# Two column blocks in turn and a bias by running sum: one change to a two-layer hybrid decoder kernel

## The chip, the cores and the metric

The kernel runs on one core of one Trainium2 chip. The time is the device time of one execution in microseconds; the figure to be predicted is the median over the runs of the changed kernel. Before the change three runs took 926.28, 926.46 and 927.83 us, so the median is 926.46.

The core has five engines that each work through a queue of their own in order: TensorE (PE) multiplies matrices into the accumulator memory PSUM, VectorE (DVE) and ScalarE (ACT) work element by element, GpSimd (POOL) here does a few small things and starts transfers, SyncE (SP) starts transfers. They wait for each other by semaphores.

## The reference

Two layers (DEPTH = 2) on x of 256 tokens by 2048 columns, all in float32. Each layer normalises x, multiplies it by one wide matrix w_in, and feeds the columns to four head groups of 512 columns with four heads each. The groups' outputs, each gated, are joined and multiplied by w_out (2048 x 2048), and the result is added to x.

```python
for l in range(DEPTH):
    h = rms_norm(x, norm_g[l]);  p = split_columns(h @ w_in[l])
    log_f = log_sigmoid(p["fox_f"] + fox_fb[l])          # (256, 4 heads)
    cum = cumsum(log_f, over tokens)
    # group 0, FoX: logit[t, s] = q_t.k_s / sqrt(128) + cum[t] - cum[s], causal, softmax, times v
    # group 1: difference of two softmax maps; group 2, MoBA: here plain causal attention
    # group 3, GLA: gated linear attention
    mixed = concat(group outputs, each times silu(gate))
    x = x + mixed @ w_out[l]
return rms_norm(x, final_norm_g)
```

With 256 tokens the MoBA group has a single block of keys, so it is plain causal attention with rotary positions. What matters for the change is the bias of FoX: the row t gets cum[t] added on all of its keys, and a softmax along a row doesn't feel what is the same on the whole row. So any form of the bias will do that has the right differences along s.

## The kernel before

**Steps.** All weights lie in DRAM in the order in which they are used. `_blocks` (L96) lists the column blocks: for each layer 17 blocks of w_in, then 4 blocks of w_out of 512 columns (the last one of the second layer is cut). `_steps` (L131) cuts every block into steps along the 2048 rows: a step of a 512-column block is two tiles of 128 rows, so a block has eight steps. In a w_out block the row tiles come in the order of the groups 3, 0, 1, 2 (GLA, FoX, difference, MoBA); the group that is finished last, MoBA, fills the last two steps. A block with a `turn` shares its time with others of the same turn: the first few blocks of each layer go quarter by quarter, since their input arrives by quarters. The blocks of w_out had no turn.

**One step.** SP loads 512 KB of weights into one of four buffers `raw`. ACT copies it, rounded to the format that PE multiplies fast, into `hi` (L401), DVE subtracts to get the rest `lo` (L404); four buffers of each. PE then makes twelve matmuls of 512 columns (`multiply`, L1192): for two row tiles and two halves of the tokens, hi weights by hi and lo input, lo weights by hi input. `prepare` runs three steps ahead of `multiply`. The sums of a block stay in one of two PSUM buffers `mm`; when the block is complete, its `done` function drains it. For w_out that is `residual` (L1015): in layer 0 the first two blocks are copied to xs by ACT and x is added later by a DMA, all others are added to xs by DVE. Then `make_hT` (L434) turns the new x for the next layer by way of DRAM, in passes that are counted.

**Tasks.** Everything else (rotary, softmax, GLA, splitting the results) is written as generators in the list `tasks`. After each step `tick` (L258) goes once over the list and lets each task run to its next `yield`; it breaks off when a rough account of DVE or ACT time says that these have more than their share, the account being filled by PE's work. So the order on every engine is settled when the program is written. If a step needs a group that no task has finished (`need`, L1288), passes are forced until it is there, without steps between them.

**Turns through DRAM.** `moved` (L297) writes a tile to DRAM from POOL's queue, yields, reads it back in four parts from the same queue, and then yields LAND = 5 times before anything uses it. `gate` of MoBA, q and k of all groups go this way.

**The tail of a group.** `attend_columns` (L791) waits for v and for the turned gate, yields, multiplies by v into a PSUM buffer `side` (two of these, shared by all tasks), yields, multiplies by the gate on DVE, yields, and `split_group` (L526) makes hi (ACT), yields, and lo (DVE): the tiles mTh and mTl.

**The bias before.** `fox_first` (L840) takes the four gate columns out of PSUM (`fx`, 128 tokens x 2 x 4 heads, bias fb added). `fox_forget` (L858) makes their log-sigmoid, times sqrt(128), splits it into hi and lo, and scales a constant 0/1 triangle by each of the columns (16 ACT copies); DVE spreads the second half's values over 128 columns. The class `Forget` (L819) then adds the bias by eight products with 0/1 matrices (`upto_r`, `ones_r`) into the same PSUM sums as q by k; `softmax` (L722) calls it ahead of each set of scores. After that DVE adds the causal mask `neg4` to the diagonal parts.

**GLA** (`gla`, L612) works in two pairs of heads; in each, DVE fills `ee` and `tq`, and 28 PE products (L685) take both `side` buffers.

Of the kernel before, what the change touches and what calls it, by code (L numbers as in the profile page):

```python
# [21 lines left out]
P = 128  # L22
# [4 lines left out]
H = 4  # L27
# [36 lines left out]
def _constants():  # L64

    i = np.arange(P)
    tables, at = {"f": [], "b": []}, {}

    def put(name, a, kind="f"):
        parts = tables[kind]  # L70
        at[name] = (sum(x.shape[1] for x in parts), a.shape[1])
        parts.append(np.ascontiguousarray(a, TYPES[kind]))

    put("ident", np.eye(P))
    put("after", (i[:, None] > i[None, :]))
    for name, half in (("rot_d", DIFF_HALF), ("rot_m", MOBA_HALF)):
        rot = 2 * half
        inv = np.float32(500000.0) ** (-np.arange(0, rot, 2, dtype=np.float32) / np.float32(rot))
        ang = np.arange(SEQ, dtype=np.float32)[:, None] * inv[None, :]
        cos, sin = np.cos(ang), np.sin(ang)  # L80
        both = np.concatenate([cos, cos, -sin, sin], 1).reshape(2, P, 4 * half)
        put(name, both.transpose(1, 0, 2).reshape(P, -1))
    put("upto", (i[:, None] <= i[None, :]), "b")
    put("neg", np.where(i[None, :] > i[:, None], NEG, 0.0), "b")
    masks = []
    for h in GLA_LEVELS:
        blk, second = i // (2 * h), (i // h) % 2 == 1
        masks.append(((blk[:, None] == blk[None, :]) & ~second[:, None])[:, second])
    put("masks", np.concatenate(masks, 1), "b")
    return {k: np.concatenate(v, 1) for k, v in tables.items()}, at  # L90
# [5 lines left out]
def _blocks():  # L96

    def block(w, l, c0, n, kind, groups=(0, 1, 2, 3), turn=None):
        kts = [g * 4 + i for g in groups for i in range(4)]
        return {"w": w, "l": l, "c0": c0, "n": n, "kind": kind, "kts": kts, "per": 4 if n * 4 <= STEP_W else 2, "turn": turn}  # L100

    out = []
    for l in range(DEPTH):
        for i, (c0, n) in enumerate((
            (COL["gla_a"], 264),
            (COL["gla_q"], 512),
            (COL["gla_g"] + 248, 264),
            (COL["gla_v"], 512),
            (COL["fox_v"] + 258, 258),
            (COL["fox_q"], 512),  # L110
            (COL["fox_k"], 512),
            (COL["diff_q"], 512),
            (COL["diff_k"], 512),
            (COL["fox_v"], 258),
            (COL["fox_g"], 512),
            (COL["diff_v"], 512),
            (COL["moba_q"], 512),
            (COL["moba_k"], 512),
            (COL["diff_g"], 512),
            (COL["moba_g"], 512),  # L120
            (COL["moba_v"], 512),
        )):
            out.append(block("w_in", l, c0, n, "rows", turn=l if i in ((0, 1, 2), (0, 2))[l] else None))
        for chunk in range(4):
            cut = l + 1 == DEPTH and chunk == 3
            out.append(block("w_out", l, chunk * 512, 256 if cut else 512, "rows", (3, 0, 1, 2)))
    out.append(block("w_out", DEPTH - 1, D - 256, 256, "apart", (3, 0, 1, 2)))
    return out


def _steps():  # L131

    steps, first = [], {}
    for i, b in enumerate(_blocks()):
        per, turn = b["per"], b["turn"]
        for j in range(0, KT, per):
            key = (i, 0, 0) if turn is None else (first.setdefault(turn, i), j // 4, i)
            steps.append((key, len(steps), {"block": i, "kts": b["kts"][j:j + per], "first": j == 0, "last": j + per == KT}))
    steps = [s for _, _, s in sorted(steps, key=lambda z: z[:2])]
    at = 0  # L140
    for s in steps:
        s["at"] = at
        at += P * len(s["kts"]) * _BLOCKS[s["block"]]["n"]
    return steps
# [61 lines left out]
def hybrid_trunk(  # L206
# [107 lines left out]
        return ct[:, o:o + n]  # L314

    ident = cst("ident")
    after = cst("after")
    turns = {k: cst(k).rearrange("p (m z w) -> p m z w", m=2, z=2) for k in ("rot_d", "rot_m")}
    masks = cp.tile([P, NL, 64], U8, name="masks")
    fb = cp.tile([P, DEPTH, H], F32, name="fb")  # L320
    gain = cp.tile([P, 2, DEPTH], F32, name="gain")
    wa = cp.tile([17, DEPTH, 256], F32, name="wa")
    upto_r = cp.tile([P, P], F32R, name="upto_r")
    ones_r = cp.tile([P, P], F32R, name="ones_r")
    neg_b = cp.tile([P, P], BF16, name="neg_b")
    neg4 = neg_b[:, None, :].to_broadcast([P, H, P])
    halfpow = cp.tile([P, 8], F32, name="halfpow")
# [21 lines left out]
    def constants():  # L349
# [3 lines left out]
        nc.scalar.dma_start(wa[16:17].rearrange("p l e -> p (l e)"), gla_ba.rearrange("(o l) e -> o (l e)", o=1))  # L353
        yield
        s = []
        for name in ("upto", "masks"):
            c, n = CAT[name]
            s.append(s4.get([P, n], BF16))
            nc.scalar.dma_start(s[-1], const_b[:, c:c + n])
        yield  # L360
        c, n = CAT["neg"]
        nc.scalar.dma_start(neg_b, const_b[:, c:c + n])
        nc.scalar.dma_start(fb.rearrange("p l h -> p (l h)"), bcast_rows(fox_fb, 0, DEPTH * H))
        yield
        lamt = s2.get([P, DEPTH, 4, 64])
        nc.scalar.dma_start(lamt.rearrange("p l a d -> p (l a d)"), bcast_rows(diff_lam, 0, DEPTH * 256))
        nc.scalar.dma_start(gain, norms_t)
        yield
        v_.tensor_copy(upto_r, s[0])
        v_.tensor_copy(masks.rearrange("p l t -> p (l t)"), s[1])  # L370
        v_.tensor_scalar(ones_r, ident, 0.0, 1.0, op0=OP.mult, op1=OP.add)
        s4.put(*s)
        ready.add("constants")
        yield
# [237 lines left out]
    def gla(l, an):  # L612
# [34 lines left out]
        for pair in range(2):  # L647
# [32 lines left out]
            v_.tensor_mul(ee[:, 0, NL], ee[:, 0, NL], kv[:, 0])  # L680
            v_.tensor_mul(ee[:, 1, NL], ee[:, 1, NL], qv[:, 1])
            yield
            both = yield from take_both()
            pcs = [z.rearrange("p (l x c) -> p l x c", l=NL + 1, x=2) for z in both]
            for m in range(2):  # L685
# [36 lines left out]
    def softmax(qT, kT, scale, su, forget):  # L722
# [3 lines left out]
        for m in range(2):  # L726
            for kt in range(m + 1):
                dst = S[m][:, kt]
                if forget is not None:
                    forget(dst, m, kt)  # L730
                for h in range(H):
                    matmul(dst[:, h], qT[:, m * H + h], kT[:, :, kt * H + h],
                           forget is None, forget is None or h == H - 1)
        s4.put(qT, kT)
        if forget is not None:
            forget.release()
        yield
        p = []
        for m in range(2):
            v_.tensor_add(S[m][:, m], S[m][:, m], neg4)  # L740
            mx = sm.tile([P, H], F32, name="mx")
            if m == 0:
                v_.tensor_reduce(mx, S[0][:, 0], axis=AX.X, op=OP.max)
# [72 lines left out]
        yield  # L816
        yield from split_group(l, gi, mixed, lambda: s4.put(mixed))

    class Forget:  # L819


        def __init__(self):
            self.fg, self.f1 = [], []

        def __call__(self, dst, m, kt):
            fg, f1 = self.fg, self.f1
            if m == kt:
                matmul(dst, upto_r, fg[0][:, m], True, False)
                matmul(dst, upto_r, fg[1][:, m], False, False)
            else:  # L830
                matmul(dst, ones_r, fg[0][:, 0], True, False)
                matmul(dst, ones_r, fg[1][:, 0], False, False)
                matmul(dst, upto_r, f1[0], False, False)
                matmul(dst, upto_r, f1[1], False, False)

        def release(self):
            s4.put(*self.fg)
            s2.put(*self.f1)

    def fox_first(l, ps):  # L840
        r = env["r", l]
        vn = s4.get([P, 2, GW])
        fx = sm.tile([P, 2, H], F32, name="fx", bufs=2)
        for m in range(2):
            v_.scalar_tensor_tensor(fx[:, m], ps[m][:, 254:258], r[:, m:m + 1], fb[:, l], op0=OP.mult, op1=OP.add)
            a_.activation(vn[:, m, 258:], ps[m][:, :254], AF.Copy, scale=r[:, m:m + 1])
        env["fox_v", l] = vn
        env["forget", l] = Forget()
        tasks.append(fox(l))
        tasks.append(fox_forget(l, fx, env["forget", l]))  # L850

    def fox_v(l, ps):
        r, vn = env["r", l], env["fox_v", l]
# [1 line left out]
            a_.activation(vn[:, m, :258], ps[m], AF.Copy, scale=r[:, m:m + 1])  # L855
        ready.add(("fox_v", l))

    def fox_forget(l, fx, forget):  # L858
        yield
        e = sm.tile([P, 2, H], F32, name="fe", bufs=2)  # L860
        f = sm.tile([P, 2, H], F32, name="f", bufs=2)
        yield from log_sigmoid(f, fx, e)
        v_.tensor_scalar(f, f, math.sqrt(HD), None, op0=OP.mult)
        yield
        fh = sm.tile([P, 2, H], F32R, name="fh", bufs=2)
        fl = sm.tile([P, 2, H], F32R, name="fl", bufs=2)
        hi_of(fh, f)
        lo_of(fl, f, fh)
        yield
        for part in (fh, fl):  # L870
            z = yield from s4.take([P, 2, H, P], F32R)
            pf = part.bitcast(F32)
            for m in range(2):
                for h in range(H):
                    a_.activation(z[:, m, h], after, AF.Copy, scale=pf[:, m, h:h + 1])
                yield
            forget.fg.append(z)
            y = yield from s2.take([P, H, P], F32R)
            v_.tensor_copy(y, pf[:, 1, :, None].to_broadcast([P, H, P]))
            forget.f1.append(y)  # L880
            yield
        ready.add(("forget", l))

    def fox(l):
# [443 lines left out]
```

## Time and profile before

| what | value |
| --- | --- |
| median of three runs | 926.46 us (926.28 to 927.83) |
| time of the profiled execution | 925.78 us |
| its span, first to last instruction | 924.0 us |
| granted TensorE clock, mean | 0.994 |
| matmuls | 4694 |
| HBM read, written | 178.79 MB, 15.20 MB |
| DMA mean over the span | 211 GB/s |

In the rows of a profile, L12 is line 12 of the kernel; nearly all ACT and DVE rows have L176 and nearly all matmuls L277, the lines of the helpers that record them, so they are told apart by their tiles ("out<-in"). "x24" is a count. A float32 matmul of 128 columns counts as two records. A bracket holds the idle time just before an instruction and who ended it. Matmuls overlap, so start times tell PE's pace better than durations do.

### The profile page before, as it was taken

The page shows a single profiled execution, that of the slowest core. Times are in us where ns is not written, and L with a number is a line of the kernel's source. Part 1 is how long each engine was busy: PE and PEld are TensorE (multiplying, and loading weights), DVE is VectorE, ACT ScalarE, POOL GpSimd, SP SyncE. Part 2 cuts the span into 40 slices and gives each one's busy share as a digit, 9 for nine tenths or more (in the row PEclk, how much of TensorE's full clock was granted, in tenths as well). Part 3 has the DMA queues.
Part 4 walks back from the last instruction along what each step waited for, and adds up shares of the span by engine and source line. Part 5 has one row for each costly group of instructions (what it writes and reads, how often), then busy time and mean ns, then how long its engine had stood idle before and what let it go on. Part 6 is the DMA issues. An engine that isn't in the chain of part 4 may idle for free.

```text
span 924.0 us, 12695 instructions
## 1 busy us (share of the span) xinstructions
PE 907.0 (98%) x4694; PEld 771.5 (83%) x4694; DVE 625.6 (68%) x967; ACT 506.4 (55%) x712; POOL 88.9 (10%) x145
## 2 busy tenths in 40 slices
PE   9999999999999999899999999999999999998996
PEld 7989888898888888788898887888888888887886
DVE  7656777787569578556755549867975885694562
ACT  6576773374554466346656575743645545743441
POOL 1010002220001121001200100012110012110000
PEclk9999999999999999999999999999999999999999
DMA  8776557767657768578855845867776576694652
GB/s 320 245 241 190 182 176 260 248 204 229 209 177 230 228 189 235 170 202 261 289 178 164 256 150 178 242 190 247 225 232 178 167 243 207 203 290 147 201 160 92
DMA packets 56865, 194.84 MB, mean 211 GB/s; under 512 B 8001, under 2 KB 8289, under 8 KB 56802
## 3 DMA queue, kind: packets, MB, share of 16 engines
q1 hardware_dynamic: 46048, 164.20, 55.6%
q0 software_dynamic: 9264, 28.32, 10.8%
q10 hardware_dynamic: 1490, 1.51, 0.6%
q8 instruction: 37, 0.61, 0.3%
q14 instruction: 26, 0.21, 0.1%
HBM read 178.79 MB, written 15.20 MB: 210 GB/s over the span
## 4 chain that ended last, share of the span: by engine, by line
PE 95%; DVE 2%; ACT 1%; issue 1%; DMA 0%; POOLq 0%; POOL 0%; DVEq 0%; SPq 0%; ACTq 0%
PE mm L277 86%; PE side L277 9%; ACT eight L176 0%; DMA four<-in_xt 0%; DVE tq L176 0%; DVE lo L176 0%; ACT hi L176 0%; DVE mTl L176 0%; DVE four L176 0%; ACT mTh L176 0%; DVE xs L176 0%; ACT L176 0%; PE side L281 0%; DVE hTp L176 0%; POOLq L1324 0%
## 5 line engine op out<-in xcount | busy, mean ns | idle before, releaser
L176 DVE TENSOR_TENSOR lo<-raw,hi 128x1024 fp32r<-128x1024 f32 (+3 forms) x301 | 364.6, 1220 | 251.8 <-ACT hi L176 250.3
L176 ACT ACTIVATE hi<-raw 128x1024 fp32r<-128x1024 f32 (+3 forms) x301 | 317.1, 1059 | 362.3 <-PE mm L277 310.0
L277 PE MATMUL mm<-hi,hTp 128*128 128x512 f32 (+2 forms) x2048 | 465.1, 371 | 0.0
L277 PEld LDWEIGHTS mm<-hi,hTp 128*128 128x128 f32 x2048 | 358.3, 188 | 66.0 <-ACT hi L176 1.0
L277 PE MATMUL mm<-lo,hTp 128*128 128x512 f32 (+2 forms) x1024 | 249.8, 369 | 0.1
L277 PEld LDWEIGHTS mm<-lo,hTp 128*128 128x128 f32 x1024 | 181.1, 188 | 32.8 <-DVE lo L176 0.3
L277 PE MATMUL mm<-hi,mTh 128*128 128x512 f32 (+1 forms) x256 | 96.7, 382 | 4.8 <-ACT mTh L176 4.8
L277 PE MATMUL mm<-hi,mTl 128*128 128x512 f32 (+1 forms) x256 | 97.0, 383 | 1.5 <-DVE mTl L176 1.5
L277 PE MATMUL mm<-lo,mTh 128*128 128x512 f32 (+1 forms) x256 | 64.4, 376 | 0.0
L277 PEld LDWEIGHTS mm<-hi,mTh 128*128 128x128 f32 x256 | 49.0, 192 | 14.0 <-ACT mTh L176 5.2
L277 PEld LDWEIGHTS mm<-hi,mTl 128*128 128x128 f32 x256 | 49.2, 192 | 11.2 <-DVE mTl L176 2.1
L304 POOL DMA_DIRECT2D four<-turn x84 | 46.0, 553 | 102.2 <-DMA turn<-four 43.5
L277 PEld LDWEIGHTS mm<-lo,mTh 128*128 128x128 f32 x256 | 46.4, 189 | 8.9
L301 POOL DMA_DIRECT2D turn<-four x21 | 12.2, 582 | 407.9 <-DVE four L176 407.9
L176 DVE STREAM_TRANSPOSE pT<-four 32x128 f32<-32x128 f32 (+1 forms) x116 | 39.3, 350 | 1.0
L176 ACT ACTIVATE four<-mm,rstd 128x512 f32<-128x512 f32 (+2 forms) x56 | 33.6, 648 | 3.6 <-DVE fx L176 3.6
L176 ACT ACT_TABLE_LOAD x24 | 30.8, 1283 | 3.3 <-DVE an L176 3.0
L277 PEld LDWEIGHTS side<-four,four 128*128 128x128 f32 (+1 forms) x224 | 22.0, 190 | 2.3 <-issue 1.4
L277 PE MATMUL side<-four,four 128*128 128x128 f32 (+1 forms) x224 | 23.3, 277 | 0.0
L176 DVE STREAM_TRANSPOSE four<-four 128x1024 f32<-128x1024 f32 x18 | 22.4, 1245 | 0.3
L176 ACT ACTIVATE four<-side,nb 128x256 f32<-128x256 f32 (+1 forms) x48 | 20.5, 444 | 0.6 <-DVE nb L176 0.6
L176 DVE COPY_PREDICATED four<-masks,side 128x128 f32<-128x128 uint8 x56 | 19.0, 340 | 1.8
(145 smaller groups left out, 545.1 us busy)
## 6 DMA issues: line engine op xcount, KB each, us to landing
raw<-in_weights SPq DMA_DIRECT2D x272, 512.0 KB, 4.1
turn<-four POOLq DMA_DIRECT2D x21, 512.0 KB, 5.0
four<-turn POOLq DMA_DIRECT2D x84, 128.0 KB, 4.4
raw<-in_weights SPq DMA_DIRECT2D x16, 516.0 KB, 4.9
raw<-in_weights SPq DMA_DIRECT2D x15, 528.0 KB, 4.9
turn<-gate POOLq DMA_DIRECT2D x4, 512.0 KB, 4.8
gate<-turn POOLq DMA_DIRECT2D x16, 128.0 KB, 5.3
four<-in_xt SPq DMA_DIRECT2D x3, 512.0 KB, 7.1
```

The lines of the kernel that those rows point to most:

```text
L176: return f(*args, **kw)
L277: t_.matmul(out, lhsT, rhs, start=start, stop=stop)
L301: g_.dma_start(via, t.rearrange("p c a b -> p c (a b)"))
L304: g_.dma_start(t[c * 32:(c + 1) * 32].rearrange("p q a b -> p q (a b)"), via[:, c].rearrange("(q i) e -> i q e", q=4))
```

## The change

Three things are changed.

The first two blocks of w_out of each layer get a turn of their own with one cut, at row tile 12 of 16: first twelve row tiles (six steps) of block 0, then six steps of block 1, then the last two steps of block 0 and the last two of block 1. Blocks 2 and 3 follow as before.

FoX's bias is made in another way. PE transposes fx to four rows of 256 tokens, DVE adds fb (now one value per row), the log-sigmoid follows, DVE makes a running sum along the 256 keys and scales it by -sqrt(128). POOL's queue writes these 4 KB to DRAM and reads them back spread over 128 partitions (512 KB). DVE adds the causal mask to both diagonal parts in SBUF. In the softmax DVE adds the three resulting tiles to the scores, where it used to add the mask to two parts; the eight 0/1 products, the class Forget and the constants `after`, `upto` and `ones_r` are gone.

gla() gets one more yield in each pair, between its last multiplications on DVE and its taking both side buffers.

```diff
-            out.append(block("w_in", l, c0, n, "rows", turn=l if i in ((0, 1, 2), (0, 2))[l] else None))
+            out.append(block("w_in", l, c0, n, "rows", turn=(l, (4, 8, 12)) if i in ((0, 1, 2), (0, 2))[l] else None))
         for chunk in range(4):
             cut = l + 1 == DEPTH and chunk == 3
-            out.append(block("w_out", l, chunk * 512, 256 if cut else 512, "rows", (3, 0, 1, 2)))
+            out.append(block("w_out", l, chunk * 512, 256 if cut else 512, "rows", (3, 0, 1, 2),
+                             turn=(DEPTH + l, (12,)) if chunk < 2 else None))
...
-            key = (i, 0, 0) if turn is None else (first.setdefault(turn, i), j // 4, i)
+            key = (i, 0, 0) if turn is None else (first.setdefault(turn[0], i), sum(j >= c for c in turn[1]), i)
...
-    fb = cp.tile([P, DEPTH, H], F32, name="fb")
+    fb = cp.tile([H, DEPTH], F32, name="fb")
...
             v_.tensor_mul(ee[:, 1, NL], ee[:, 1, NL], qv[:, 1])
             yield
+            yield
             both = yield from take_both()
...
                 dst = S[m][:, kt]
-                if forget is not None:
-                    forget(dst, m, kt)
                 for h in range(H):
-                    matmul(dst[:, h], qT[:, m * H + h], kT[:, :, kt * H + h],
-                           forget is None, forget is None or h == H - 1)
+                    matmul(dst[:, h], qT[:, m * H + h], kT[:, :, kt * H + h], True, True)
...
-            v_.tensor_add(S[m][:, m], S[m][:, m], neg4)
+            if forget is None:
+                v_.tensor_add(S[m][:, m], S[m][:, m], neg4)
+            elif m == 0:
+                v_.tensor_add(S[0][:, 0], S[0][:, 0], forget[0])
+            else:
+                for j, z in enumerate(forget[1:]):
+                    v_.tensor_add(S[1][:, j], S[1][:, j], z)
+                s4.put(env["forget tile"])
+                s2.put(forget[0])
...
-            v_.scalar_tensor_tensor(fx[:, m], ps[m][:, 254:258], r[:, m:m + 1], fb[:, l], op0=OP.mult, op1=OP.add)
+            v_.tensor_scalar(fx[:, m], ps[m][:, 254:258], r[:, m:m + 1], None, op0=OP.mult)
...
+    def fox_forget(l, fx):
+        yield
+        ps = yield from take_side()
+        for m in range(2):
+            transpose(ps[0:H, m * P:(m + 1) * P], fx[:, m])
+        yield
+        z = yield from s2.take([P, SEQ])
+        e = yield from s2.take([P, SEQ])
+        v_.tensor_scalar(z[:H], ps[:H, :SEQ], fb[:, l:l + 1], None, op0=OP.add)
+        side.put(ps)
+        yield
+        yield from log_sigmoid(z[:H], z[:H], e[:H])
+        v_.tensor_tensor_scan(e[:H], z[:H], z[:H], 0.0, op0=OP.add, op1=OP.bypass)
+        v_.tensor_scalar(z[:H], e[:H], -math.sqrt(HD), None, op0=OP.mult)
+        s2.put(e)
+        yield
+        via = dram.tile([H, SEQ], F32, name="sums", tag="sums", bufs=2)
+        g_.dma_start(via, z[:H])
+        s2.put(z)
+        yield
+        t = yield from s4.take([P, H, SEQ])
+        g_.dma_start(t, via[None, :, :].to_broadcast([P, H, SEQ]))
+        for _ in range(LAND):
+            yield
+        first = yield from s2.take([P, H, P])
+        v_.tensor_add(first, t[:, :, :P], neg4)
+        v_.tensor_add(t[:, :, P:], t[:, :, P:], neg4)
+        env["forget tile"] = t
+        env["forget", l] = first, t[:, :, :P], t[:, :, P:]
         ready.add(("forget", l))
```

More of the change, by code (lines that the diff above doesn't have):

```diff
@@ L74, in _constants @@
     put("ident", np.eye(P))
-    put("after", (i[:, None] > i[None, :]))
     for name, half in (("rot_d", DIFF_HALF), ("rot_m", MOBA_HALF)):
@@ L82, in _constants @@
         put(name, both.transpose(1, 0, 2).reshape(P, -1))
-    put("upto", (i[:, None] <= i[None, :]), "b")
     put("neg", np.where(i[None, :] > i[:, None], NEG, 0.0), "b")
@@ L316, in hybrid_trunk @@
     ident = cst("ident")
-    after = cst("after")
     turns = {k: cst(k).rearrange("p (m z w) -> p m z w", m=2, z=2) for k in ("rot_d", "rot_m")}
     masks = cp.tile([P, NL, 64], U8, name="masks")
-    fb = cp.tile([P, DEPTH, H], F32, name="fb")
+    fb = cp.tile([H, DEPTH], F32, name="fb")
     gain = cp.tile([P, 2, DEPTH], F32, name="gain")
     wa = cp.tile([17, DEPTH, 256], F32, name="wa")
-    upto_r = cp.tile([P, P], F32R, name="upto_r")
-    ones_r = cp.tile([P, P], F32R, name="ones_r")
     neg_b = cp.tile([P, P], BF16, name="neg_b")
@@ L355, in constants @@
         s = []
-        for name in ("upto", "masks"):
+        for name in ("masks",):
             c, n = CAT[name]
@@ L362, in constants @@
         nc.scalar.dma_start(neg_b, const_b[:, c:c + n])
-        nc.scalar.dma_start(fb.rearrange("p l h -> p (l h)"), bcast_rows(fox_fb, 0, DEPTH * H))
+        nc.scalar.dma_start(fb, bass.AP(tensor=fox_fb.tensor, offset=fox_fb.offset, ap=[[1, H], [H, DEPTH]]))
         yield
@@ L368, in constants @@
         yield
-        v_.tensor_copy(upto_r, s[0])
-        v_.tensor_copy(masks.rearrange("p l t -> p (l t)"), s[1])
-        v_.tensor_scalar(ones_r, ident, 0.0, 1.0, op0=OP.mult, op1=OP.add)
+        v_.tensor_copy(masks.rearrange("p l t -> p (l t)"), s[0])
         s4.put(*s)
@@ L728, in softmax @@
                 dst = S[m][:, kt]
-                if forget is not None:
-                    forget(dst, m, kt)
                 for h in range(H):
-                    matmul(dst[:, h], qT[:, m * H + h], kT[:, :, kt * H + h],
-                           forget is None, forget is None or h == H - 1)
+                    matmul(dst[:, h], qT[:, m * H + h], kT[:, :, kt * H + h], True, True)
         s4.put(qT, kT)
-        if forget is not None:
-            forget.release()
         yield
@@ L817, in attend_columns @@
         yield from split_group(l, gi, mixed, lambda: s4.put(mixed))
[L819 to L838, printed above, removed]
     def fox_first(l, ps):
@@ L844, in fox_first @@
         for m in range(2):
-            v_.scalar_tensor_tensor(fx[:, m], ps[m][:, 254:258], r[:, m:m + 1], fb[:, l], op0=OP.mult, op1=OP.add)
+            v_.tensor_scalar(fx[:, m], ps[m][:, 254:258], r[:, m:m + 1], None, op0=OP.mult)
             a_.activation(vn[:, m, 258:], ps[m][:, :254], AF.Copy, scale=r[:, m:m + 1])
         env["fox_v", l] = vn
-        env["forget", l] = Forget()
         tasks.append(fox(l))
-        tasks.append(fox_forget(l, fx, env["forget", l]))
+        tasks.append(fox_forget(l, fx))
     def fox_v(l, ps):
@@ L856, in fox_v @@
         ready.add(("fox_v", l))
-    def fox_forget(l, fx, forget):
+    def fox_forget(l, fx):
         yield
[L860 to L863, printed above, removed]
+        ps = yield from take_side()
+        for m in range(2):
+            transpose(ps[0:H, m * P:(m + 1) * P], fx[:, m])
         yield
[L865 to L868, printed above, removed]
+        z = yield from s2.take([P, SEQ])
+        e = yield from s2.take([P, SEQ])
+        v_.tensor_scalar(z[:H], ps[:H, :SEQ], fb[:, l:l + 1], None, op0=OP.add)
+        side.put(ps)
         yield
[L870 to L880, printed above, removed]
-            yield
+        yield from log_sigmoid(z[:H], z[:H], e[:H])
[10 more added lines that the diff above has]
+        for _ in range(LAND):
+            yield
+        first = yield from s2.take([P, H, P])
[3 more added lines that the diff above has]
+        env["forget", l] = first, t[:, :, :P], t[:, :, P:]
         ready.add(("forget", l))
```

## The prediction

> **What bounds the kernel now.** I read the page first (busy times and the chain of waits), then the waits of PE, then the PE timeline around each wait.
>
> ```profile
> span 924.0 us, 12695 instructions
> PE 907.0 (98%) x4694; PEld 771.5 (83%) x4694; DVE 625.6 (68%) x967; ACT 506.4 (55%) x712; POOL 88.9 (10%) x145
> ...
> PE 95%; DVE 2%; ACT 1%; issue 1%; DMA 0%; POOLq 0%; POOL 0%; DVEq 0%; SPq 0%; ACTq 0%
> ```
>
> PE sets the time nearly everywhere. Only two things can move it: fewer matmuls, or fewer moments in which PE stands still. The waits of PE name the second:
>
> ```profile
> PE mm L277 <- ACT mTh L176: 4.8, 2, 2.4
> PE mm L277 <- DVE mTl L176: 1.5, 2, 0.8
> PE side L342 <- DVE four L337: 1.3, 1, 1.3
> PE side L277 <- DVE eight L176: 0.8, 1, 0.8
> ```
>
> The first two rows are one event in each layer, the third is the start of the program, the fourth a place in layer 1. The PE timeline shows what each costs (start, us, what; the bracket is the idle time before):
>
> ```profile
> 332.50 2.84 PE L277 MATMUL side<-four,four 128*128 128x128 f32 x24
> ...
> 337.03 1.08 PE L277 MATMUL mm<-lo,hTp 128*128 128x512 f32 x4
> 337.95 1.98 PE L277 MATMUL mm<-hi,hTp 128*128 128x512 f32 x8
> 339.76 1.07 PE L277 MATMUL mm<-lo,hTp 128*128 128x512 f32 x4
> 340.67 1.98 PE L277 MATMUL mm<-hi,hTp 128*128 128x512 f32 x8
> ...
> 381.47 2.84 PE L277 MATMUL side<-pT,four 128*128 128x128 f32 x24
> 386.71 0.51 PE L277 MATMUL mm<-hi,mTh 128*128 128x512 f32 x1 [2.40 <-ACT mTh L176]
> 387.97 0.80 PE L277 MATMUL mm<-hi,mTl 128*128 128x512 f32 x1 [0.76 <-DVE mTl L176]
> ...
> 391.06 1.07 PE L277 MATMUL mm<-lo,mTh 128*128 128x512 f32 x4
> ...
> 835.61 2.84 PE L277 MATMUL side<-pT,four 128*128 128x128 f32 x24
> ...
> 845.12 1.09 PE L277 MATMUL mm<-lo,mTh 128*128 128x512 f32 x4
> ```
>
> An undisturbed step is 2.72 us (337.95 to 340.67): 1.81 of "hi" matmuls, 0.91 of "lo". From the start of 24 side matmuls to the next "lo" it is 337.03 - 332.50 = 4.53. Around the wait in layer 0 the same work takes 391.06 - 381.47 = 9.59, in layer 1 845.12 - 835.61 = 9.51. So **each stall costs 5.06 and 4.98 us, together 10.04**, although PE is idle for only 2.40 + 0.76 = 3.16. The rest is a slow clock behind it: from 387.97 the last seven of the eight hi matmuls take 3.09 us to the next lo, 0.44 each, where eight in 1.81 are 0.23 each, and the window view (columns: span, busy time of PE, PEld, DVE, ACT, POOL, granted clock, DMA share, GB/s) has a clock of 0.76:
>
> ```profile
> 384.00:391.10 7.10, 3.94 (x12) 2.82 (x12) 2.45 (x2) 1.06 (x1) 0.00 (x0) 0.76 0.25 76
> ```
>
> **Part 1, two column blocks in turn.** The stall is the tail of the MoBA group. Its product with v (24 side matmuls), the gating, the split into hi and lo follow each other with nothing between, just ahead of the seventh step of the first w_out block, which needs them:
>
> ```profile
> 384.35 1.22 DVE L176 TENSOR_TENSOR four<-side,gate 128x1024 f32<-128x1024 f32 x1 [1.27 <-PE side L277]
> 386.69 1.23 DVE L176 TENSOR_TENSOR mTl<-four,mTh 128x1024 fp32r<-128x1024 f32 x1 [1.12 <-ACT mTh L176]
> ...
> 385.60 1.06 ACT L176 ACTIVATE mTh<-four 128x1024 fp32r<-128x1024 f32 x1 [3.78 <-DVE four L176]
> ...
> 356.79 2.18 POOL L304 DMA_DIRECT2D gate<-turn  x4 [2.92 <-DMA turn<-gate]
> ```
>
> The new order puts six steps of the second block ahead of that seventh step: 6 x 2.72 = 16.3 us and six passes of tick(). The tail needs five passes once the gate's turned tile counts as ready (attend_columns: one yield, product, gating, hi, lo). The gate's reads were issued at 356.79, nine steps before 381.47, and need five passes; passes that break off on the DVE budget can eat four of the nine. If none is owed, the tail ends one pass before it is needed, two steps ahead of PE; with one owed, in time still, because DVE runs ahead of PE. I cost the stall at nothing from here: gain 10.04. The other end is that all passes are still forced: gain 0.
>
> What is late next: the first block ends after 14 of the pair's 16 steps, 6 steps later than now (the last quarters of both stand at the end), so both PSUM buffers of "mm" are open at once, and the third block needs the first one's buffer two steps (5.44 us) after its last matmul. Draining it takes two instructions, behind one hi or one lo:
>
> ```profile
> L176 ACT ACTIVATE hi<-raw 128x1024 fp32r<-128x1024 f32 x268 | 282.7, 1061 | 324.4 <-PE mm L277 281.9 <-DMA raw<-in_weights 13.8 <-DVE four L176 6.4
> ...
> L176 DVE TENSOR_TENSOR lo<-raw,hi 128x1024 fp32r<-128x1024 f32 x268 | 325.0, 1221 | 221.4 <-ACT hi L176 220.2
> ...
> L176 DVE TENSOR_TENSOR xs<-mm,xs 128x512 f32<-128x512 f32 x10 | 6.4, 682 | 0.0
> ```
>
> Layer 1 (DVE): 1.22 + 2 x 0.68 = 2.6 us; layer 0 does it on ACT, whose copy of that size I take as no longer than DVE's: 1.06 + 1.36 = 2.4. Spare 2.8 us. I take 0; if it is missed by another 5 us of work ahead on that engine, PE idles 2.2 and loses about 3.6 by the ratio above (5.02 for 3.16). Then make_hT(0) of layer 0, with its x accumulation and turn on POOL's queue, starts 6 steps later than now, one block less ahead of make_hT(1), which keeps its place; layer 1's first steps come 18 steps (49 us) after the first block's end, and 13 passes are needed. Cost 0. Bytes of weights are the same, only their order differs.
>
> **Part 2, the bias.** Eight matmuls of 512 columns per layer go:
>
> ```profile
> 176.84 0.64 PE L277 MATMUL side<-four,upto_r 128*128 128x512 f32 x2
> ...
> 183.24 1.08 PE L277 MATMUL mm<-lo,hTp 128*128 128x512 f32 x4
> ...
> 636.42 0.64 PE L277 MATMUL side<-four,upto_r 128*128 128x512 f32 x2
> ...
> 642.82 1.08 PE L277 MATMUL mm<-lo,hTp 128*128 128x512 f32 x4
> ...
> 58.42 0.22 PE side L281 x2
> ```
>
> From the first forget matmul to the next "lo" is 6.40 us in both layers; MoBA's scores, the same without bias, take 4.53. Gain 2 x 1.87 = 3.74. Added are two transposes per layer, like the pair of GLA's in the last row: 2 x 0.22 = 0.44 of PE. Net gain 3.30, all of it on PE's path.
>
> The other engines:
>
> ```profile
> L176 ACT ACTIVATE four<-ct,fh 128x128 fp32r<-128x128 f32 x16 | 5.1, 389 | 0.0
> ...
> L176 DVE TENSOR_TENSOR side<-side,neg_b 128x512 f32<-128x512 f32 x12 | 8.3, 690 | 0.6 <-PE side L277 0.6
> ...
> L176 DVE TENSOR_TENSOR_SCAN two<-two 128x128 f32<-128x128 f32 x8 | 2.7, 404 | 0.0
> L176 DVE COPY at<-side 16x256 f32<-16x256 f32 x2 | 0.8, 405 | 0.0
> ...
> L176 DVE CAST two<-fh 128x512 fp32r<-128x512 f32 x2 | 0.8, 419 | 0.0
> ```
>
> ACT loses 16 scaled copies per layer (some 5 us). DVE loses two casts (0.84) and a few tiny instructions (about 0.5); it gains two mask additions in SBUF and one more on the scores (3 x 0.69), three passes over 4x256 (about 0.41 each, estimated from the 16x256 copy) and a scan of 256 (at most 2 x 0.404): 4.1. Net about +2.8 us of DVE per layer. It hides under PE, since DVE is 68% busy; uncovered it would cost 2 x 2.8 = 5.6.
>
> The way through DRAM is new on POOL's queue: a 4 KB write, then a broadcast read of 512 KB that waits for it. Behind them on that queue stand the turns of fox_q and fox_k, for which the projections' tasks count six passes (16.3 us). No row has this broadcast; the nearest are a 512 KB write and the broadcast of final_norm_g:
>
> ```profile
> turn<-four POOLq DMA_DIRECT2D x21, 512.0 KB, 5.0
> two<-in_final_norm_g POOLq DMA_DIRECT2D x4, 256.0 KB, 7.3
> ```
>
> The read is issued one pass (2.72 us) after the write, so it leaves at most 2.3 us late and lands 9.6 us after its pass; DVE's additions come five passes (13.6 us) after it. Spare 4.0 us. Twice 7.3 for twice the bytes would be 3.3 us late; the usual lead of DVE over PE (three steps, 8.2 us, less 2.3 for hi and lo) covers that. A turn held up behind them for the 5.0 us of the write still has room: two transfers of 5.0 in 16.3. I take 0 for all of it. The constants that go (a table of 64 KB, two small DVE instructions, half of a load on ACT's queue) stood beside the first blocks; 0.
>
> **Part 3, one more yield in gla().** The fourth wait:
>
> ```profile
> 561.64 1.07 PE L277 MATMUL mm<-lo,hTp 128*128 128x512 f32 x4
> 563.47 3.39 PE L277 MATMUL side<-tq,eight 128*128 128x128 f32 x28 [0.76 <-DVE eight L176]
> ```
>
> The side matmuls could have begun at 561.64 + 0.91 = 562.55; 0.92 us are lost because DVE is less than one step behind. A pass more is 2.72 us: gain 0.92, between 0 and 0.92. GLA's later end (two passes per layer) is far ahead of w_out.
>
> **Sum.** 10.04 + 3.30 + 0.92 = 14.26. The profiled execution took 925.78 us (span 924.0 and 1.78 around it): 911.52. The median of the runs is 0.68 above it, so 912.2.
>
> **A rule weighed.** The row first: PE idled 3.16 us in two pieces and the clock fell to 0.76 over the next microseconds. The Trainium skill, page "TensorE: Matmul & The Clock Gate" (What's actually happening; HAM oscillation), says the clock halves after an idle window of about 3.4 us and that gaps need only be kept below that. By that rule a wait this short would not by itself slow the clock, the slow stretch could have another cause and stay, and the sum would keep only the idle time. The trace disagrees as far as it goes: both stalls show the slow stretch, and it begins right behind them.
>
> **Rivals.** *The stall stays or moves (13%).* The tail is forced all the same, or the third block waits for its buffer. For: passes can break off on the budget, and both buffers are open. Against: 16.3 us of cover, 2.8 spare. One layer kept: 917.2; both: 922.2; buffers late in both layers by 3.6: 919.4.
> *The slow clock stays (4%).* Only the idle 2 x 3.16 = 6.32 of the 10.04 is won: 912.2 + 3.7 = 915.9. Against: the 0.76 us wait at 563.47 had no slow matmuls behind it, the longer ones had.
> *DVE work comes uncovered (3%).* 912.2 + 5.6 = 917.8.
> *Slower: the broadcast lands late (4%).* DVE works in order; waiting for the bias it holds back every "lo" behind it, and PE stops in fox's stage of each layer. It begins to cost when the read takes over 13.6 - 2.3 + 5.9 = 17.2 us, and eats the whole gain at about 5.3 us of idle (7.1 lost with the slow clock) per layer, so from 22.5 us on. At 25 us: 7.8 idle and 1.9 of slow clock, 9.7 per layer: 912.2 + 19.4 = 931.6. For: 128 partitions read the same 4 KB. Against: final_norm_g's broadcast does that too, at 7.3.
>
> **Chances.** The forecast holds at 76%. Below it little can lie: the remaining PE waits are the program's start, so 910.0 allows 2 us for what I rounded and for the runs' own spread. Above, 917.5 takes in one stall kept, the clock and the DVE case; it leaves out the two stalls kept, the late buffers and the slower case, some 12%, and what I haven't seen. About 0.2% (1.9 us) is what can be told from no change; faster: 95%, within: 1%, slower: 4%.
>
> **What would show it.** Right: no PE wait on mTh or mTl in the waits, the 24 matmuls of side<-pT between two steps of block 1 of w_out, granted clock 1.00 there; no groups with upto_r and ones_r, two transposes out of fx per layer; no wait of PE on "eight"; the first lo after fox's scores 4.5 us after their start. Wrong: PE waiting on the draining of mm (ACT or DVE xs) at the third block, a DVE wait on the broadcast's DMA with PE idle behind it, or new waits of PE on "lo" in the stages of GLA and FoX.

## The result and the profile after

Four executions of the changed kernel took 911.41, 912.68, 917.53 and 917.98 us, median 915.11; before, four took 926.00 to 927.83, median 926.37. The ratio is 0.987, 95% interval 0.984 to 0.990: faster by 1.3%. The forecast was 912.2 with a range of 910.0 to 917.5. The four times are two pairs some 5 us apart, and the forecast met the lower one. The median 915.11 is the mean of 912.68 and 917.53, a time that no execution took; with three long ones of four it would have left the range, so that it lies inside is partly luck. Most of what follows is about the gap.

The profiled execution took 912.68 us, 13.10 less than that of before. Busy times from its page:

```profile
PE 899.6 (99%) x4682; PEld 766.5 (84%) x4682; DVE 630.8 (69%) x969; ACT 498.0 (55%) x678; POOL 91.4 (10%) x149
```

The waits of PE, all of them:

```profile
PE side L338 <- DVE four L333: 1.3, 1, 1.3
PE side L280 <- issue: 1.0, 1, 1.0
PE side L280 <- DVE xs L175: 0.2, 1, 0.2
```

The rows on mTh, mTl and "eight" are gone; the program's start is left, and a new place has come: the eight transposes (L280) of the last quarter of x between the layers, which wait 1.02 and 0.25 us. The PE timeline of the same profile shows the places that the sum was made of:

```profile
179.36 2.84 PE L276 MATMUL side<-four,four 128*128 128x128 f32 x24
...
183.89 1.08 PE L276 MATMUL mm<-lo,hTp 128*128 128x512 f32 x4
...
384.84 2.84 PE L276 MATMUL side<-pT,four 128*128 128x128 f32 x24
...
389.34 1.07 PE L276 MATMUL mm<-lo,mTh 128*128 128x512 f32 x4
...
561.88 1.07 PE L276 MATMUL mm<-lo,hTp 128*128 128x512 f32 x4
562.79 3.29 PE L276 MATMUL side<-tq,eight 128*128 128x128 f32 x28
...
830.22 2.84 PE L276 MATMUL side<-pT,four 128*128 128x128 f32 x24
...
834.72 1.07 PE L276 MATMUL mm<-lo,mTh 128*128 128x512 f32 x4
```

From MoBA's product with v to the next lo it is 4.50 us in both layers (9.59 and 9.51 before), FoX's scores take 4.53 (6.40), and GLA's products follow their step after exactly the 0.91 us of its lo. So the gains stand: 10.10, 3.74 less the new transposes, 0.92. The new place takes some of it back. The PE timeline at the change of layers, after and then before:

```profile
457.66 1.14 PE L276 MATMUL side<-lo,hTp 128*128 128x264 f32 x8
459.82 0.30 PE L280 MATMUL side<-ct,xs 128*128 128x128 f32 x1 [1.02 <-issue]
460.37 0.98 PE L280 MATMUL side<-ct,xs 128*128 128x128 f32 x7 [0.25 <-DVE xs L175]
...
464.13 2.09 PE L276 MATMUL side<-hi,hTp 128*128 128x264 f32 x16
```

```profile
464.82 1.14 PE L277 MATMUL side<-lo,hTp 128*128 128x264 f32 x8
465.80 1.04 PE L281 MATMUL side<-ct,xs 128*128 128x128 f32 x8
...
469.58 2.09 PE L277 MATMUL side<-hi,hTp 128*128 128x264 f32 x16
```

The same work takes 464.13 - 457.66 = 6.47 us where it took 4.76: 1.71 lost. With 14.26 forecast, 1.71 lost here and some 0.4 won in the program's first 15 us (the first side matmuls of a step start at 14.70, before at 15.13), 12.95 of the measured 13.10 are accounted for.

Why DVE is late with xs is read from POOL's timeline, after and then before:

```profile
424.16 0.58 POOL L300 DMA_DIRECT2D turn<-four  x1 [12.03 <-DVE four L175]
428.02 2.23 POOL L303 DMA_DIRECT2D four<-turn  x4 [3.28 <-PE mm L276]
430.23 0.57 POOL L300 DMA_DIRECT2D turn<-four  x1
437.91 2.33 POOL L303 DMA_DIRECT2D four<-turn  x4 [7.11 <-DMA turn<-four]
440.27 0.56 POOL L300 DMA_DIRECT2D turn<-four  x1
449.18 2.19 POOL L303 DMA_DIRECT2D four<-turn  x4 [8.35 <-DMA turn<-four]
```

```profile
414.98 0.60 POOL L301 DMA_DIRECT2D turn<-four  x1 [17.35 <-DVE four L176]
421.27 2.20 POOL L304 DMA_DIRECT2D four<-turn  x4 [5.69 <-PE mm L277]
...
437.17 0.60 POOL L301 DMA_DIRECT2D turn<-four  x1 [12.45 <-DVE four L176]
443.37 2.22 POOL L304 DMA_DIRECT2D four<-turn  x4 [5.61 <-DMA turn<-four]
445.58 0.56 POOL L301 DMA_DIRECT2D turn<-four  x1
453.58 2.19 POOL L304 DMA_DIRECT2D four<-turn  x4 [7.43 <-DMA turn<-four]
```

Each pair of rows is the turn of one quarter of x through DRAM: a write, then reads that wait until it has landed. Before, the reads of the first quarter were issued 16 us ahead of the second's write. Now all three stand one behind the other on POOL's queue. The second quarter's reads are issued 7.7 us after its write (6.2 before). The third quarter's write stands behind them:

```profile
435.30 2.16 DVE L175 STREAM_TRANSPOSE four<-xs 128x512 f32<-128x512 f32 x2
```

DVE had this tile ready at 437.46, and POOL issued the write at 440.27, 2.8 us later; before the change that gap was 1.0 us (444.62 to 445.58). ACT, whose passes were counted for less, waits for the turned tiles in order with everything behind it:

```profile
447.45 2.84 ACT L175 ACTIVATE hTp<-four,ngt 128x256 fp32r<-128x256 f32 x4 [5.12 <-DMA four<-turn]
...
453.87 2.98 ACT L175 ACTIVATE hTp<-four,ngt 128x256 fp32r<-128x256 f32 x4 [0.65 <-DMA four<-turn]
```

The rows are the second and the third quarter. ACT's hi, DVE's lo and with them the addition to xs (in order behind lo) come later, and PE meets its transposes too early.

### The profile page after: what moved, and what is told of

Read it like the earlier page. It is cut to its first block, busy times and chain, and to the rows that moved or that the text cites. A ratio compares the mean times of both kernels' runs of the same rounds, so it can differ in the third digit from the quotient of the medians.

```text
span 910.9 us, 12657 instructions
## 1 busy us (share of the span) xinstructions
PE 899.6 (99%) x4682; PEld 766.5 (84%) x4682; DVE 630.8 (69%) x969; ACT 498.0 (55%) x678; POOL 91.4 (10%) x149
## 4 chain that ended last, share of the span: by engine, by line
PE 97%; issue 1%; DMA 0%; DVE 0%; SPq 0%; POOLq 0%; POOL 0%; ACT 0%; DVEq 0%; ACTq 0%
PE mm L276 89%; PE side L276 9%; DMA four<-in_xt 0%; DVE xs L175 0%; PE side L280 0%; DVE lo L175 0%; POOLq L1305 0%; POOL rf L393 0%; ACT two L175 0%; DVE hTp L175 0%; SPq L1091 0%; DVEq L1305 0%; SPq L1089 0%; DVE ssf L175 0%; DVE pw L175 0%
## 5 line engine op out<-in xcount | busy, mean ns | idle before, releaser
L276 PE MATMUL mm<-hi,mTl 128*128 128x512 f32 (+1 forms) x256 | 95.0, 376 | 0.0
```

Source lines behind the costliest of these rows:

```text
L276: t_.matmul(out, lhsT, rhs, start=start, stop=stop)
```

## The experiments

Theory A: the long executions lose their 5 us at the change of layers, when the wait there grows long enough for the clock to fall. Rivals: the bias's way through DRAM (B), the chip (C), another place (D).

**The same kernel again.**

> The changed kernel as it is, more executions. Its first four lay in two groups, 911.4 and 912.7 us (clock 0.998), 917.5 and 918.0 us (clock 0.994). Theory A: the larger time is a stall of PE at the change of layers, where the eight transposes of x (side<-ct,xs) waited 1.3 us in the profiled execution because ACT had waited 5.1 us for a DMA four<-turn and DVE was late with xs; when that wait is longer, the clock drops and the whole costs some 5 us more. Then the groups appear again, 911 to 913 and 917 to 918. Rival B: the variation sits in the bias's way through DRAM, and the profile shows PE waiting in fox's stage. Rival C: it was the chip of that job, and all executions here lie in one group.

912.46, 917.51, 911.41, 913.35, 914.38 us; ratio 0.986 (0.984 to 0.988). The spread returns, with times between the groups too: not two fixed times but a loss of varying size. The profiled execution (912.46) had 0.6 us of waiting at the transposes. C falls.

**The turn in one layer only.**

```diff
-turn=(DEPTH + l, (12,)) if chunk < 2 else None))
+turn=(DEPTH + l, (12,)) if chunk < 2 and l == 1 else None))
```

A second run has l == 0 in its place.

> w_out's first two blocks in turn in layer 1 alone, layer 0 in the old order; bias and yield as changed. Theory A: one group, 912 + 5.1 = 917 us (the stall of layer 0's w_out is back), no wait of PE at side<-ct,xs, all executions within 1.5 us. Rival B or C: still two groups some 5 us apart, near 917 and 922.

916.53, 916.78, 918.95, 919.20 us (0.990, 0.989 to 0.992). The stall of layer 0's w_out is back with 2.4 and 0.8 us, there is no wait at the transposes, and nothing lies near 922. That the four would lie within 1.5 us was wrong: they spread by 2.7. The executions of the kernel before, on the same chip, spread by 4.1 (924.16 to 928.26).

> In turn in layer 0 alone. Theory A: two groups, 912 + 5.0 = 917 and 922 to 923 us. If the variation needs layer 1's turn, one group at 917. The stall of layer 1's w_out is back, 5.0 us, none in layer 0's.

916.78, 916.85, 919.05, 920.03, 922.56, 922.62 us (0.993, 0.991 to 0.995): with the turn in layer 0 the times reach 5.8 us up, as A says. The profiled one (916.85) shows the stall kept in layer 1 and the clock behind it. Columns: stretch, its length, busy time of PE, PEld, DVE, ACT, POOL, granted clock, DMA share, GB/s:

```profile
829.00:834.20 5.20, 2.04 (x8) 1.35 (x7) 2.45 (x2) 1.06 (x1) 0.00 (x0) 0.97 0.31 101
834.20:837.40 3.20, 3.20 (x9) 2.47 (x8) 0.27 (x1) 1.06 (x1) 0.00 (x0) 0.51 0.02 5
```

The idle 3.16 us end at 832.85; the clock falls to half for about 3.2 us, and here it does so 1.4 us after the work has resumed. In the kernel before it fell at once, at 387.97 (0.52 from 387.9 to 391.1 us). So in these profiles the slow stretch follows the wait, and its start varies.

**The transposes one pass later.**

```diff
         if chunk == 3:
             yield
+            yield
             ps = yield from take_side()
```

> The changed kernel with one more yield ahead of the transposes of x's last quarter, so that PE has one more step (2.9 us) before it meets them. Theory A: the 1.3 us wait is gone, the group near 917 goes or becomes rare, times 910 to 912. If ACT's wait of 5 us also makes the weights' hi late, a wait appears one step later instead and the two groups stay. Rival B or C: two groups as before.

911.70, 912.45, 912.63, 912.99 us (0.984, 0.983 to 0.986), a little above the 910 to 912 expected, and no wait of PE but the start's. ACT still waited 5.6 us for four<-turn in the profiled one. One more step of cover in front of the transposes, and no execution is long. Four without a long one could be chance (four of the eleven executions of the changed kernel in this document are above 917), but the four of the run without the pause, below, have the same extra yield and stay under 914.5. The place is right.

**The transposes one pass earlier** (the changed kernel's one yield taken out).

```diff
         if chunk == 3:
-            yield
             ps = yield from take_side()
```

> The changed kernel with one yield less ahead of the transposes of x's last quarter: PE meets them one step (2.9 us) earlier, so the wait of 0.6 to 1.3 us becomes 3.5 to 4.2 us in every execution. Theory A: the clock falls behind it, 912 + 2.9 + about 2 = 917 us in all executions, the time of the long group. Rival D: 915 and 920, that is 2.9 us on both groups.

915.32, 916.49, 916.84, 918.36 us (0.988, 0.986 to 0.991). PE waits 4.3 us on xs in the profiled one (918.36 us); no execution is short any more. The median, 916.66, is what A gave within 0.4, and D's 920 doesn't occur. But the four spread by 3.0 us, and the lowest is what D gave its short group; the two profiles that come next part A from D.

**Two more profiled executions of the changed kernel.**

> One more profiled execution of the changed kernel, in the hope of one near 917. Theory A: if it is long, PE waits at the eight transposes side<-ct,xs (or at the first step behind them) for more than 2 us and the granted clock falls there; if it is short, the wait is under 1.5 us. Rival D: a long execution has the same wait at the change of layers and loses its 5 us elsewhere.

> Another profiled execution of the changed kernel, with the same expectations as the first look: a long one has more than 2 us of waiting at the change of layers and a lower clock behind it, a short one under 1.5 us.

The first took 918.95 us, the second 911.57. The long one's PE timeline:

```profile
458.08 1.14 PE L276 MATMUL side<-lo,hTp 128*128 128x264 f32 x8
464.04 2.31 PE L280 MATMUL side<-ct,xs 128*128 128x128 f32 x8 [4.82 <-issue]
466.00 3.53 PE L276 MATMUL mm<-hi,hTp 128*128 128x264 f32 x16
...
470.33 2.11 PE L276 MATMUL side<-hi,hTp 128*128 128x264 f32 x16
```

The stretch from 455 to 470 us in the long and then in the short one (columns as above):

```profile
455.00:470.00 15.00, 10.07 (x65) 9.60 (x64) 9.06 (x13) 7.68 (x12) 0.00 (x0) 0.77 0.62 200
```

```profile
455.00:470.00 15.00, 15.00 (x127) 15.00 (x126) 11.00 (x14) 9.33 (x15) 0.00 (x0) 1.00 0.74 225
```

4.82 us of waiting, then transposes and the next hi at a slower pace (2.31 and 3.53 us where they take 1.04 and 2.1). From 458.08 to 470.33 it is 12.25 us against 4.76: 7.49 lost, and the two executions differ by 7.38. So the whole difference is here: A holds, D falls. PE's releaser reads "issue" in that row; what is behind it stands in the timelines of POOL and ACT of the long execution:

```profile
440.61 2.33 POOL L303 DMA_DIRECT2D four<-turn  x4 [7.18 <-DMA turn<-four]
442.96 0.56 POOL L300 DMA_DIRECT2D turn<-four  x1
450.89 2.18 POOL L303 DMA_DIRECT2D four<-turn  x4 [7.36 <-DMA turn<-four]
```

```profile
447.21 2.86 ACT L175 ACTIVATE hTp<-four,ngt 128x256 fp32r<-128x256 f32 x4 [4.46 <-DMA four<-turn]
...
458.31 2.76 ACT L175 ACTIVATE hTp<-four,ngt 128x256 fp32r<-128x256 f32 x4 [5.32 <-DMA four<-turn]
```

Behind the last row follow ACT's hi, DVE's lo and xs, and the transposes. It is the third quarter that is late. ACT starts on the second one 0.9 us later than in the short execution (446.30 there), on the third 5.95 us later (452.36 there, after 0.29 us of waiting). The third quarter lost a little at each step: its write stood 5.1 us on POOL's queue behind the second quarter's reads (2.9 in the short execution), its reads were issued 7.9 us after it (6.7), and ACT used them 7.4 us after that (4.8). In the first two POOL waits for a write to land. Why the reads themselves took longer stays open; weights loaded at the same time were slow too (6.15 us in the chain of waits, landing at 458.51).

**The turn off POOL's queue earlier.** x for the first block is loaded by SP ahead of time and added by DVE.

```diff
-            if l == 0 and chunk < 2:            # residual: copy, x added later by a DMA
+            if l == 0 and chunk == 1:
...
-        if l == 1 and chunk < 2:                # make_hT: the DMA that adds x, four passes
+        if l == 1 and chunk == 1:
...
-        if i in X_AT[2:]:
+        if i in X_AT and i != X_AT[1]:
```

> The changed kernel, but x for the first block of columns is loaded ahead by SP and added by DVE in layer 0, as for the third and fourth block, in place of a copy by ACT and a DMA that adds; its turn through DRAM then starts about five passes (13 us) earlier and is off POOL's queue before the second block's begins. Theory A with POOL's queue as the cause: ACT's wait for four<-turn falls from 3 to 5 us to under 1, no wait at side<-ct,xs, no execution above 914, median 911.5 to 912.5. Rival (the transposes wait because the passes of three quarters crowd ACT and DVE, not because of POOL): wait and long group stay.

910.88, 911.27, 911.34, 911.50, 911.61 and one 914.70 us; median 911.42, ratio 0.983 (0.981 to 0.986). POOL's timeline:

```profile
410.93 0.57 POOL L300 DMA_DIRECT2D turn<-four  x1 [53.72 <-DVE four L175]
416.16 2.18 POOL L303 DMA_DIRECT2D four<-turn  x4 [4.66 <-DMA turn<-four]
...
431.41 0.60 POOL L300 DMA_DIRECT2D turn<-four  x1 [11.78 <-DVE four L175]
435.34 2.20 POOL L303 DMA_DIRECT2D four<-turn  x4 [3.34 <-DMA turn<-four]
```

The reads of the first turn are issued 13 us before the second begins, the third quarter's write is issued 0.6 us after DVE has its tile ready (437.82 to 438.38), ACT's longest wait for four<-turn is 1.7 us (under 1 was expected), PE does not wait at the transposes. So the turns standing one behind the other cause the late transposes. The edit also takes the first quarter's passes on ACT and DVE ahead and a copy off ACT, so by itself it doesn't part POOL's queue from crowded engines; ACT's longest waits in this stage, which are for the DMA four<-turn, speak for the queue. The one 914.70, above the 914 expected as a limit, was not profiled and stays open.

**The parts alone.** First the bias without the turn and without the second yield in gla().

> Only the new bias: w_out in the old order, no second yield in gla(). Theory: the scores of FoX take 4.53 us to the next lo instead of 6.40 in both layers, two pairs of transposes of 0.22 come, nothing else: 926.4 - 3.3 = 923.1 us, both stalls of w_out (2.40 + 0.76 us) still there. Rival (DVE work or the way through DRAM comes uncovered): between 924 and 932, with new waits of PE in fox's stage. If the wait of PE on eight was caused by the old bias's ACT work, it is gone here without the yield, 922.2.

922.43 us median of ten (920.95 to 925.04) beside 927.25 before; ratio 0.994 (0.993 to 0.996), 5 us with an interval from 3.5 to 6.9. Then the order alone.

> Only the new order of w_out's first two blocks; the old bias. Theory: 926.4 - 10.0 = 916.4 us, none of the stalls of w_out, the wait of 0.8 us on eight still there; some executions up to 5 us longer through the change of layers (wait at the transposes side<-ct,xs). Rival (the new bias is what makes the variation): all executions near 916.

915.43, 915.60, 916.98, 919.46, 920.49, 922.21, 922.47 us; 0.991 (0.988 to 0.994). The long executions come without the new bias: B falls (the profiled one was short, so their place was not seen in this run). The waits of PE beside the program's start, first with the bias alone, then with the order alone:

```profile
PE mm L275 <- ACT mTh L174: 4.8, 2, 2.4
...
PE mm L275 <- DVE mTl L174: 1.2, 2, 0.8
PE side L279 <- DVE xs L174: 0.3, 1, 0.3
```

```profile
PE side L277 <- DVE eight L176: 0.8, 1, 0.8
```

Each part removes its own waits. But "eight" is gone with the bias alone, with no second yield there.

**Passes or time?** Only four steps of the second block ahead of the first one's last quarter (and the transposes one pass later).

```diff
-turn=(DEPTH + l, (12,)) if chunk < 2 else None))
+turn=(DEPTH + l, (12,) if chunk == 0 else (8,)) if chunk < 2 else None))
```

> As the kernel with the transposes one pass later, but only four steps of the second block of w_out stand ahead of the first block's last quarter. Theory of the prediction (five passes for the tail, counted from the gate): in layer 0 only lo of MoBA's tail is forced, PE waits about 2.4 us for mTl there and not for mTh; layer 1, whose product comes one pass earlier, has no wait. Time 912.5 + 2.4 to 4.4 (with a slow clock) = 915 to 917. Rival: the cover is a matter of time and not of passes (four steps are 10.9 us for a tail of 6.2), no wait at all, 912.5.

914.32, 914.37, 915.40, 916.21 us (0.986, 0.983 to 0.990). The PE timeline in layer 0:

```profile
396.49 0.72 PE L276 MATMUL mm<-hi,mTl 128*128 128x512 f32 x1 [2.46 <-DVE mTl L175]
```

Of MoBA's tail PE waits for lo alone, in layer 0 alone, for the time expected: four steps are one pass too few there. In the next 3.3 us the clock was 0.54.

**The bias without its pause** (and the transposes one pass later).

```diff
         g_.dma_start(t, via[None, :, :].to_broadcast([P, H, SEQ]))
-        for _ in range(LAND):
-            yield
```

> As the kernel with the transposes one pass later, but the mask additions follow the issue of the bias's broadcast at once, without the five passes. Theory (DVE runs up to 5.9 us ahead of PE, the broadcast of 5.9 us follows a write of 3.0): DVE waits for the DMA some 3 to 4 us in each layer, PE does not wait: 912.5 us, the same. Rival (DVE's lead is not there in fox's stage): PE waits 3 us or more per layer, 916 to 922.

913.33, 913.60, 914.13, 914.41 us (0.985, 0.982 to 0.988), 1.3 us above the kernel with the pause (medians, on two different chips). A wait of DVE, then one of PE:

```profile
DVE two L175 <- DMA four<-sums: 10.2, 2, 5.7
```

```profile
PE side L276 <- DVE four L175: 2.2, 2, 1.2
```

DVE stood still for 10.2 us in two waits, more than the 3 to 4 us each that I gave; PE for 2.2 of it. Its lead covers four fifths, not all.

## Why the prediction was right, and where it was not

**The stalls of w_out.** Right in place, size and mechanism: 10.04 forecast, 10.10 in the profile. The account by passes is shown by the run with four steps. In layer 1 the product came behind the second block's first step, one step earlier than in layer 0, so there is a pass more to spare there than I counted.

**The clock behind a wait.** Counting the slow stretch into the stall was right: the stall kept in one layer shows it at 0.51. The page "TensorE: Matmul & The Clock Gate" of the Trainium skill (What's actually happening) has a half rate and a window of 3.4 us that runs freely; the trace agrees with the half, with a stretch of about 3.2 us, and with a start that varies. It disagrees with the need for an idle window of that length: 2.40 and 0.76 us with one matmul between, and 2.46 us in one piece, were enough; 1.02 and 0.25 us (the profiled execution of the changed kernel, clock 1.00 from 455 to 470 us) were not.

**The bias.** 1.87 us per layer as forecast. DVE's busy time rose by 5.2 us (630.8 against 625.6) where 5.6 was forecast, and PE has no wait for it. The way through DRAM was off the critical path, as costed, and its prices in this profile were below my bounds:

```profile
four<-sums POOLq DMA_DIRECT2D x2, 512.0 KB, 5.9
...
sums<-two POOLq DMA_DIRECT2D x2, 4.0 KB, 3.0
```

The bounds were 5.0 for the write and 7.3 to 14.6 for the broadcast. The price of losing its cover, which the slower rival took from DVE's lead of 5.9 us, was a little kind: the run without the pause lost 1.1 us of PE per layer at waits of that length.

**The second yield.** The 0.92 us are won, but the cause I named is not shown. With the bias alone the wait was gone too, and with the order alone it stayed. That points to the old bias's work on ACT and DVE in that stage, but no run takes the two apart, and whether the yield alone would also remove the wait was not tried.

**The step that failed** is the sentence on make_hT(0): that it starts six steps later, one block less ahead of make_hT(1), at "Cost 0". I compared passes with passes (13 needed, 18 there) and left out that the turns share POOL's queue, where a read waits for its write and blocks the next turn. I had named the queue, but priced it only for the bias. The term is 0 to 1.7 us in the profiled short executions and about 7.5 in the profiled long one, most of it through the third quarter, whose turn the sum did not look at. The rival "the stall stays or moves" had its price in sight (917 to 922), but named the other handover, the PSUM buffer of the third block; no run showed a wait there. Its price for late buffers has a small slip: 2.2 us idle at 5.02 for 3.16 make 3.5, not 3.6. The two long executions of the first four, 917.53 and 917.98, lie just above the range's upper end, and the median inside it.

## What to carry to other kernels

When work is moved later to cover a stall, list every queue on which it now meets what used to come after it: a counted number of passes protects only as long as each transfer finds its queue free. Here waits of PE long enough for the clock to fall cost some 1.6 times their length (5.02 us for 3.16, 7.49 for 4.82), so a tight place makes times scatter by several us; several executions are needed to see it, and a profile of a long one to place it. Loading one input early, so that one turn is over before the next begins, gave the lowest median (911.42 us, ratio 0.983); the transposes one pass later (912.54, 0.984) can't be told from it.

## What was not expected of the hardware

A gap of 2.46 us on PE was followed by 3.3 us at a clock of 0.54, 1.27 us in two pieces by no slow stretch. After 3.16 us in two pieces the slow stretch began at once in one profile and 1.4 us after the work's return in another, and lasted about 3.2 us. A varying start could be behind the spread of kernels that keep a stall (916.5 to 919.2 with one, 924.2 to 928.3 for the kernel before), but no profile of both ends of such a spread was taken, so this is argued, not shown.
